# An encoder layer on one core: where the MLP's raw weights are loaded, and the order of a pair's first low part

## The chip, the cores and the metric

The kernel runs on one core of a Trainium2 chip. The metric is device time in microseconds: the median of three runs is 1814.88 us (1814.13 to 1815.59). Another execution, taken with the hardware profiler, took 1813.31 us, and its span, from the first to the last instruction, is 1811.5 us.

The engines are named as in the profile: PE multiplies matrices (PEld is its weight load), DVE and POOL work on elements, ACT computes functions and casts, and SP only issues DMA transfers. Each engine goes through its own instructions in order; semaphores hold one back until what it needs is there.

## The reference

One layer of an encoder over two sequences of 512 and 1024 tokens with 1024 features, with the same weights. Cut to what matters here:

```python
h = h + jnp.concatenate([o_attn, o_pool], axis=-1) @ w_out
m = _rmsnorm(h, norm_mlp_g)
h = h + jnp.square(jax.nn.relu(m @ w_up)) @ w_down        # the MLP: 1024 -> 4096 -> 1024
gate = jax.nn.sigmoid(_rmsnorm(h, norm_ple_g) @ w_ple_gate)
h = h + gate * (p_i @ w_ple_proj)
return _rmsnorm(h, final_norm_g)
```

Ahead of it stand an input projection, attention and a pooling mixer, which the change does not touch. All is float32.

## The kernel before

**Precision and layout.** PE multiplies in a reduced float32 format, so each operand x is split into a high part (a cast on ACT) and a low part (x minus the high part, on DVE or POOL), and each product is three matmuls: high x high, high x low, low x high (`three`). The 1536 tokens are three chunks c of 512; h is kept transposed, per chunk as four tiles `h{c}{a}` of two blocks of 128 features.

**The MLP** goes over 48 pairs: three chunks times sixteen pairs g of hidden blocks (2 x 128 hidden features each). A pair multiplies m by two columns of `w_up` by Strassen's scheme with seven products, numbered 1, 6, 2, 5, 7, 3, 4 in the order they run, each of twelve matmuls of 256 columns (px, py, pz, pq in the profile). The sums of m that the scheme needs are computed beforehand by `make_m` and go through DRAM (`mo_d`, loaded as `mo`); the sums of the weights are made for each pair by `feed` (s1 to s4 on DVE, then the split: cast on ACT, low part on POOL, L786 and L787). The results are joined into c1 and c2 (additions on DVE, L858 to L880, relu and squares on ACT, L875 to L883), and r[0] and r[1] are the high and low parts of their squares, the low parts at L886 on DVE. `down` multiplies r by two rows of `w_down` (split by `split_down`, ACT at L816, POOL and DVE at L817) in four quarters of twelve matmuls of 512 columns (pd) and adds each quarter to h (L837, DVE). The quarters of a pair run between the products of the next pair, quarter 0 after product 1.

**The order of the work** is written out by hand for PE, ACT, DVE and POOL: the text calls an instruction, and that is its place on its engine. `run` calls `after(i)` behind product i, which takes one step of several generators: of `feed` (running ahead, so that the splits of the next pair begin in `after(5)`), of `split_down`, of `raise_h`, and of the `chores`. Chores are `invert`, `finishing` of the chunk before (which ends a chunk's h and prepares the gate), and `make_m` of the chunk after. At a chunk's beginning `raise_h` multiplies h by the statistic w of the norm, in eight steps on DVE (L662).

SP's order is not written out: a transfer is issued in the place that a list scheduler gives it, "not before its turn" against PE's order, and then at run time as soon as its buffer is free. Nearly all buffers come from one pool of 49 places, so a load waits until the last reader of the place's former owner is done, and an engine that writes into a place that a DMA still reads waits for that DMA.

**Names that the prediction uses.** `wur` and `wdr` are the raw up and down weights (two tiles of 512 KB per pair), `w` their split up weights, `ws` the sums, `wd` the split down weights, `w_d` the statistic in DRAM (`sqm` is the tile in which it is computed, L646), `h_d` the place in DRAM to which `spill` writes a chunk's h until its turn comes. Before, raw up weights of the next pair are loaded in step 3 of `feed`, and its raw down weights after product 2 of the pair ahead:

```python
            for i, _ in enumerate(pr.feed()):
                if i == 3 and n + 1 < len(pairs):
                    pairs[n + 1].load_up()
                yield
```

## Time and profile before

| | |
|---|---|
| median of three runs | 1814.88 us (1814.13 to 1815.59) |
| the profiled execution | 1813.31 us, span 1811.5 us |
| mean granted clock of PE | 0.995 |
| PE busy | 1759.7 us, 97% of the span |
| DVE, POOL, ACT busy | 1260.0, 1053.7 and 939.7 us |
| the MLP in the span | from 579 us to about 1624 us |
| PE busy from 560 to 660 us | 88.3 of 100 us |
| PE busy from 930 to 1040 us | 104.6 of 110 us |
| DMA, mean over the span | 142 GB/s |

A row of a timeline has the start in us, the length, the engine, the line of the kernel, the operation, what it writes and reads by the program's names without numbers, the shape, and in square brackets how long the engine stood idle before it and on what. A row of the waits has who waited for whom, us in total, how often, and the longest. "Issue" is time in which the profile shows nothing that the engine waited for. Matmuls are pipelined: a row of twelve lasts a little longer than the time until the next twelve start, and the starts give the pace.

### The profile page before, as it was taken

The numbers are of one execution on the slowest core, as the hardware profiler recorded it, in microseconds if no ns is written. First come the engines' busy times: TensorE is split into PE (matmuls) and PEld (weight loads), VectorE is DVE, ScalarE is ACT, GpSimd is POOL, SyncE is SP. The second block draws the span as 40 slices with busy tenths as digits, with TensorE's granted clock in tenths as the row PEclk, the third lists the DMA queues.
The fourth block names the chain that finished last, engine by engine and source line by source line (L and its number), as shares of the span: only waits on it lengthen the run. The fifth ranks groups of instructions, "written<-read, shape, count | busy, mean of one in ns | idle before, by whom it ended". The sixth has DMA issues, their size and how long they took to land.

```text
span 1811.5 us, 28604 instructions
## 1 busy us (share of the span) xinstructions
PE 1759.7 (97%) x10540; PEld 1537.1 (85%) x10540; DVE 1260.0 (70%) x1843; ACT 939.7 (52%) x1854; POOL 1053.7 (58%) x923
## 2 busy tenths in 40 slices
PE   9999899999999799999999999999999999999997
PEld 7888777888868798988888889889898999888887
DVE  5677865888894677865568877876776556665655
ACT  6434455768794455655445545554455444443332
POOL 3474774535674567676656776785577666543121
PEclk9999999999999899999999999999999999999998
DMA  6333545120519335343364442556443323272102
GB/s 248 114 123 105 216 165 185 36 94 13 206 46 367 139 122 198 121 177 100 136 265 157 163 151 96 195 185 235 179 157 100 110 94 99 89 262 70 59 12 82
DMA packets 83883, 256.84 MB, mean 142 GB/s; under 512 B 9888, under 2 KB 16416, under 8 KB 83744
## 3 DMA queue, kind: packets, MB, share of 16 engines
q1 hardware_dynamic: 83744, 255.02, 39.7%
q8 instruction: 83, 1.36, 0.3%
q14 instruction: 56, 0.46, 0.1%
HBM read 195.74 MB, written 59.24 MB: 141 GB/s over the span
## 4 chain that ended last, share of the span: by engine, by line
PE 78%; DVE 7%; ACT 5%; DMA 3%; issue 3%; POOL 1%; POOLq 0%; DVEq 0%; ACTq 0%; SPq 0%
PE pd L49 25%; PE z L49 7%; PE px L49 6%; PE pz L49 6%; PE pq L49 6%; PE pg L49 6%; PE py L49 4%; PE pp L49 3%; PE o L49 3%; PE tp L53 3%; PE po L49 3%; PE S L49 3%; PE pj L49 1%; DMA wur<-in_w_up_dram 1%; DVE r L886 1%
## 5 line engine op out<-in xcount | busy, mean ns | idle before, releaser
L49 PE MATMUL pd<-r,wd 128*128 128x512 f32 x2304 | 568.5, 395 | 10.8 <-DVE r L886 10.6
L49 PEld LDWEIGHTS pd<-r,wd 128*128 128x128 f32 x2304 | 419.5, 188 | 100.3 <-DVE r L886 16.1
L787 POOL TENSOR_TENSOR w<-ws,w 128x512 fp32r<-128x512 f32 x192 | 272.5, 1423 | 217.9 <-ACT w L786 206.8
L787 POOL TENSOR_TENSOR w<-wur,w 128x512 fp32r<-128x512 f32 x144 | 212.8, 1489 | 135.4 <-ACT w L786 134.4
L837 DVE TENSOR_TENSOR h<-pd,h 128x1024 f32<-128x1024 f32 x192 | 233.5, 1216 | 76.6 <-PE pd L49 76.5
L786 ACT CAST w<-ws 128x512 fp32r<-128x512 f32 x192 | 118.5, 617 | 271.1 <-DVE ws L795 241.1
L461 POOL TENSOR_SCALAR pr<-pr,rr 128x512 f32<-128x512 f32 x160 | 111.2, 705 | 134.7 <-DVE rr L456 66.8
L49 PE MATMUL z<-w,x 128*128 128x512 f32 (+1 forms) x864 | 175.7, 359 | 0.9 <-DVE w L160 0.5
L49 PEld LDWEIGHTS pz<-mo,w 128*128 128x128 f32 x1152 | 150.7, 190 | 19.3 <-issue 11.2
L49 PEld LDWEIGHTS z<-w,x 128*128 128x128 f32 x864 | 142.9, 189 | 28.0 <-ACT w L159 2.1
L49 PE MATMUL pz<-mo,w 128*128 128x256 f32 x1152 | 153.6, 283 | 10.2 <-issue 10.2
L817 DVE TENSOR_TENSOR wd<-wdr,wd 128x512 fp32r<-128x512 f32 x96 | 102.8, 1071 | 83.1 <-ACT wd L816 76.6
L49 PE MATMUL pq<-mo,w 128*128 128x256 f32 x1152 | 153.7, 283 | 1.0 <-issue 1.0
L49 PE MATMUL px<-mo,w 128*128 128x256 f32 x1152 | 152.2, 281 | 0.0
L49 PEld LDWEIGHTS px<-mo,w 128*128 128x128 f32 x1152 | 146.5, 189 | 4.0
L49 PEld LDWEIGHTS pq<-mo,w 128*128 128x128 f32 x1152 | 144.7, 191 | 1.4 <-issue 1.3
L49 PE MATMUL pg<-hg,wg 128*128 128x512 f32 (+1 forms) x768 | 141.0, 338 | 0.2
L472 ACT CAST pt<-tp 128x512 fp32r<-128x512 f32 x160 | 88.0, 591 | 88.5 <-PE tp L53 86.8
L49 PEld LDWEIGHTS pg<-hg,wg 128*128 128x128 f32 x768 | 118.6, 188 | 17.8 <-DVE hg L1128 1.0
L817 POOL TENSOR_TENSOR wd<-wdr,wd 128x512 fp32r<-128x512 f32 x96 | 131.8, 1373 | 2.6 <-DMA w_d<-sqm 2.6
L886 DVE TENSOR_TENSOR r<-c,r 128x512 fp32r<-128x512 f32 x96 | 74.7, 783 | 74.1 <-ACT c L883 46.2
L473 DVE TENSOR_TENSOR pt<-tp,pt 128x512 fp32r<-128x512 f32 x160 | 104.0, 684 | 31.4 <-ACT pt L472 31.1
(195 smaller groups left out, 3036.2 us busy)
## 6 DMA issues: line engine op xcount, KB each, us to landing
wur<-in_w_up_dram SPq DMA_DIRECT2D x96, 512.0 KB, 4.2
wdr<-in_w_down_dram SPq DMA_DIRECT2D x96, 512.0 KB, 4.4
mo_d<-mm SPq DMA_DIRECT2D x84, 256.0 KB, 2.3
mo<-mo_d SPq DMA_DIRECT2D x42, 512.0 KB, 7.7
h_d<-h SPq DMA_DIRECT2D x16, 512.0 KB, 3.0
h<-h_d SPq DMA_DIRECT2D x16, 512.0 KB, 9.9
xn<-in_xn_dram SPq DMA_DIRECT2D x12, 512.0 KB, 6.4
qs_d<-qs SPq DMA_DIRECT2D x12, 512.0 KB, 3.0
```

Of the source, the lines that this page charges most:

```text
L49: last_pe[0] = nc.tensor.matmul(*a, **k).ins
L53: last_pe[0] = nc.tensor.transpose(*a, **k).ins
L461: gp.tensor_scalar(p, p, rr, 1.0, op0=ALU.mult, op1=ALU.mult)
L472: sc.copy(self.pt[kt][:, 0], tp)
L473: ve.tensor_tensor(self.pt[kt][:, 1], tp, as32(self.pt[kt][:, 0]), op=ALU.subtract)
L786: sc.copy(t[:, 0], x)
L787: gp.tensor_tensor(t[:, 1], x, as32(t[:, 0]), op=ALU.subtract)
L817: (gp, ve)[i].tensor_tensor(lo, self.dr[i][:, h], as32(hi), op=ALU.subtract)
L837: ve.tensor_tensor(h, pd.rearrange("p (a b) -> p a b", a=2), h, op=ALU.add)
L886: ve.tensor_tensor(self.r[i][:, 1], x, as32(self.r[i][:, 0]), op=ALU.subtract)
```

## The change

It has six parts.

1. Raw up weights of pair n+1 are loaded in step 5 of `feed` and not in step 3, raw down weights of a pair at its own beginning and not in the middle of the pair ahead. Pair 1's up weights are loaded ahead of the MLP. The casts and splits of down weights move from `after` 1, 6, 2, 5 to `after` 2, 5, 7, 3 (but for the first pair), and of each tile's two low parts POOL and DVE now take one each.
2. The low part of r[0] comes ahead of `after(4)`, whose step of `feed` makes the last sums and splits of weights; that of r[1] stays behind it.
3. In `down` the loop over f stands outside that over e, so that the first six matmuls of a quarter read r[0] and the last six r[1].
4. Chunk 0's statistic stays in SBUF (`ws[0] = acc[:, 1]`) and is not written to DRAM and read again, and chunk 0's h is raised in four double steps, from `after(2)` on.
5. Chunk 2's h is written to DRAM tile by tile as its last additions are made, not by `spill`, whose wait of 16 steps goes, so that the chores behind it begin in pair 1.
6. In `finishing` a step with a square of 1024 columns and two casts becomes two steps with half of each.

```diff
@@ make_m
-        sy.dma_start(w_d[c], acc[:, 1])
+        if c:
+            sy.dma_start(w_d[c], acc[:, 1])
+        else:
+            ws[0] = acc[:, 1]
@@ spill
-        yield from wait(16 if c == 2 else 0)
@@ heads_out
-                if d == KD - 1 and p % 2:
+                if p == 5:
+                    if d % 2:
+                        sy.dma_start(h_d[c][d // 2], hT[c][d // 2])
+                elif d == KD - 1 and p % 2:
@@ split_down
-                    (gp, ve)[i].tensor_tensor(lo, self.dr[i][:, h], as32(hi), op=ALU.subtract)
+                    (gp if i == (h.start > 0) else ve).tensor_tensor(lo, self.dr[i][:, h], as32(hi), op=ALU.subtract)
@@ down
-            for e in range(2):
-                d = 2 * a + e
-                for f in range(2):
+            for f in range(2):
+                for e in range(2):
+                    d = 2 * a + e
@@ run
+            ve.tensor_tensor(self.r[0][:, 1], c1, as32(self.r[0][:, 0]), op=ALU.subtract)
             after(4)
-            for i, x in enumerate((c1, c2)):
-                ve.tensor_tensor(self.r[i][:, 1], x, as32(self.r[i][:, 0]), op=ALU.subtract)
+            ve.tensor_tensor(self.r[1][:, 1], c2, as32(self.r[1][:, 0]), op=ALU.subtract)
@@ stream
-                if i == 3 and n + 1 < len(pairs):
+                if i == 5 and 0 < n < len(pairs) - 1:
                     pairs[n + 1].load_up()
@@ ahead of the MLP
     load_mo(0, ORDER[5]), load_mo(0, ORDER[6])
+    pairs[1].load_up()
     for a in range(4):
         load_h(0, a, h_d[0][a])
@@ finishing
-            sc.activation(sq, h, AF.Square)
-            if c == 0:
-                gate_in(0, a, True)
-            yield
+            for e in range(2):
+                sc.activation(sq[:, e], h[:, e], AF.Square)
+                if c == 0:
+                    gate_in(0, a, True, (e,))
+                yield
@@ the loop over pairs
             if c:
                 for a in range(4):
                     load_h(c, a, h_d[c][a])
-            load_ms(c)
+                load_ms(c)
...
+        if n:
+            pair.load_down()
         splits = pair.split_down()
...
-            if i == 1 and n + 1 < len(pairs):
-                pairs[n + 1].load_down()
...
-            next(splits, None)
-            if raising:
+            if n == 0 or i in (2, 5, 7, 3):
+                next(splits, None)
+            for _ in range(0 if not raising else 1 if c else 0 if i in (1, 6) else 2):
                 next(raising, None)
```

What this makes of the order shows in three places. In the names below, the digits behind a tile's letters are the chunk, then the pair or the block; the last number only tells tiles apart.

**The MLP's beginning, SP.** The transfers behind the last `mo` load; before:

```order
L56 DMA h00_6357<-h_d0_0_304 128x1024
L56 DMA h01_6359<-h_d0_1_305 128x1024
L56 DMA h02_6361<-h_d0_2_306 128x1024
L56 DMA h03_6363<-h_d0_3_307 128x1024
L647 DMA w_d0_259<-sqm0_4189 128x512
L708 DMA h_d2_0_312<-h20_5526 128x1024
L708 DMA h_d2_1_313<-h21_5528 128x1024
L708 DMA h_d2_2_314<-h22_5530 128x1024
L56 DMA wur0_10_6531<-in_w_up_dram 128x1024
L56 DMA wur0_11_6532<-in_w_up_dram 128x1024
L56 DMA w0_6556<-w_d0_259 128x512
```

And in the changed kernel:

```order
L56 DMA wur0_10_6357<-in_w_up_dram 128x1024
L56 DMA wur0_11_6358<-in_w_up_dram 128x1024
L56 DMA h00_6361<-h_d0_0_304 128x1024
L56 DMA h01_6363<-h_d0_1_305 128x1024
L56 DMA h02_6365<-h_d0_2_306 128x1024
L56 DMA h03_6367<-h_d0_3_307 128x1024
L760 DMA h_d2_0_312<-h20_5526 128x1024
L760 DMA h_d2_1_313<-h21_5528 128x1024
L760 DMA h_d2_2_314<-h22_5530 128x1024
L760 DMA h_d2_3_315<-h23_5532 128x1024
L56 DMA wdr0_10_6713<-in_w_down_dram 128x1024
```

Pair 1's up weights (wur0_1) have moved ahead of h; the statistic's two transfers (w_d0, w0) are gone; the writes of chunk 2's h follow h.

**The same place, DVE,** from the first pair's addition behind product 6 (u) on; before:

```order
L858 TENSOR_TENSOR u0_0_6558<-py0_0_6587,u0_0_6558 128x256
L662 TENSOR_TENSOR h00_6357<-h00_6357,w0_6556 128x512
L817 TENSOR_TENSOR wd0_011_6583<-wdr0_01_6346,wd0_010_6582 128x512
L662 TENSOR_TENSOR h01_6359<-h01_6359,w0_6556 128x512
L866 TENSOR_TENSOR u0_0_6558<-pz0_0_6630,u0_0_6558 128x256
L793 TENSOR_TENSOR ws0_10_6644<-wur0_11_6532 128x512
```

And now:

```order
L863 TENSOR_TENSOR u0_0_6559<-py0_0_6587,u0_0_6559 128x256
L822 TENSOR_TENSOR wd0_001_6582<-wdr0_00_6345,wd0_000_6581 128x512
L822 TENSOR_TENSOR wd0_011_6584<-wdr0_01_6346,wd0_010_6583 128x512
L665 TENSOR_TENSOR h00_6361<-h00_6361,sqm0_4189 128x512 x2
L871 TENSOR_TENSOR u0_0_6559<-pz0_0_6626,u0_0_6559 128x256
L798 TENSOR_TENSOR ws0_10_6640<-wur0_11_6358 128x512
L665 TENSOR_TENSOR h01_6363<-h01_6363,sqm0_4189 128x512 x2
```

The raises (h times w, now times sqm) come in twos behind product 2 and no longer ahead of the addition into u; one more split of down weights stands ahead of them, and one less behind.

**The second chunk's beginning, SP.** Before:

```order
L56 DMA wur1_10_10009<-in_w_up_dram 128x1024
L56 DMA wur1_11_10010<-in_w_up_dram 128x1024
L56 DMA mo1_40_10013<-mo_d1_40_288 128x1024
L56 DMA mo1_41_10014<-mo_d1_41_289 128x1024
L56 DMA h10_10033<-h_d1_0_308 128x1024
L56 DMA h11_10035<-h_d1_1_309 128x1024
L56 DMA h12_10037<-h_d1_2_310 128x1024
L56 DMA h13_10039<-h_d1_3_311 128x1024
L56 DMA w1_10041<-w_d1_260 128x512
```

And now:

```order
L56 DMA h10_10022<-h_d1_0_308 128x1024
L56 DMA h11_10024<-h_d1_1_309 128x1024
L56 DMA h12_10026<-h_d1_2_310 128x1024
L56 DMA h13_10028<-h_d1_3_311 128x1024
L56 DMA w1_10030<-w_d1_260 128x512
L56 DMA wdr1_00_10032<-in_w_down_dram 128x1024
L56 DMA wdr1_01_10033<-in_w_down_dram 128x1024
L56 DMA wur1_10_10090<-in_w_up_dram 128x1024
L56 DMA wur1_11_10091<-in_w_up_dram 128x1024
```

The next pair's up weights (wur1_1) and this pair's down weights (wdr1_0, before among the mo loads) now follow the statistic w1; wur1_0, before ahead of all mo loads, now stands behind the first two of them.

**A pair in the middle (chunk 0, pair 10), ACT and PE.** ACT between product 3 and quarter 0, before:

```order
L875 ACTIVATE c0_10_8741<-c0_10_8741 128x256
L876 ACTIVATE r0_100_8742<-c0_10_8741 128x512
L877 ACTIVATE c0_10_8741<-c0_10_8741 128x512
L786 CAST w0_11_2_8912<-wur0_110_8720 128x512
L881 ACTIVATE c0_10_8741<-c0_10_8741 128x512
L882 ACTIVATE r0_101_8743<-c0_10_8741 128x512
```

And now:

```order
L880 ACTIVATE c0_10_8739<-c0_10_8739 128x256
L881 ACTIVATE r0_100_8740<-c0_10_8739 128x512
L882 ACTIVATE c0_10_8739<-c0_10_8739 128x512
L791 CAST w0_11_2_8903<-wur0_110_8791 128x512
L821 CAST wd0_1010_8813<-wdr0_101_8735 128x512
L886 ACTIVATE c0_10_8739<-c0_10_8739 128x512
L887 ACTIVATE r0_101_8741<-c0_10_8739 128x512
```

A cast of down weights now stands between the steps for c1 and those for c2. The first matmuls of quarter 0 on PE, before (r0_100 is r[0] of the pair, r0_101 r[1]):

```order
L49 MATMUL pd0_100_8983<-r0_100_8742,wd0_1000_8762 128x512 x2
L49 MATMUL pd0_100_8983<-r0_100_8742,wd0_1001_8763 128x512
L49 MATMUL pd0_100_8983<-r0_101_8743,wd0_1010_8764 128x512 x2
L49 MATMUL pd0_100_8983<-r0_101_8743,wd0_1011_8765 128x512
L49 MATMUL pd0_100_8983<-r0_100_8742,wd0_1000_8762 128x512 x2
```

And now:

```order
L49 MATMUL pd0_100_8970<-r0_100_8740,wd0_1000_8811 128x512 x2
L49 MATMUL pd0_100_8970<-r0_100_8740,wd0_1001_8812 128x512
L49 MATMUL pd0_100_8970<-r0_100_8740,wd0_1000_8811 128x512 x2
L49 MATMUL pd0_100_8970<-r0_100_8740,wd0_1001_8812 128x512
L49 MATMUL pd0_100_8970<-r0_101_8741,wd0_1010_8813 128x512 x2
```

r[1] is first read by the seventh matmul of the quarter and no longer by the fourth.

## The prediction

> **What bounds the kernel now.** I read the page first, then the waits of the engine that carries the time, then the timeline of the stretches where it waits.
>
> ```profile
> PE 1759.7 (97%) x10540; PEld 1537.1 (85%) x10540; DVE 1260.0 (70%) x1843; ACT 939.7 (52%) x1854; POOL 1053.7 (58%) x923
> ```
>
> PE is busy in all but 51.8 of the span's 1811.5 us. The change removes no instruction of PE, so it can win only what PE waits.
>
> ```profile
> PE pd L49 <- DVE r L886: 10.6, 11, 1.8
> PE pz L49 <- issue: 10.2, 3, 9.2
> ```
>
> PE's two largest waits (us in total, times, longest) lie in the MLP: 10.6 us on the low part of r, in eleven pieces, and 10.2 us ahead of products 5 and 3, nearly all in one piece. That piece is the MLP's beginning:
>
> ```profile
> 584.71 1.57 PE L49 MATMUL pq<-mo,w 128*128 128x256 f32 x12
> 595.48 2.90 PE L49 MATMUL pz<-mo,w 128*128 128x256 f32 x12 [9.20 <-issue]
> 598.18 2.76 PE L49 MATMUL pq<-mo,w 128*128 128x256 f32 x12
> 604.34 0.96 PE L49 MATMUL pd<-r,wd 128*128 128x512 f32 x3 [1.77 <-DVE r L886]
> 606.04 2.12 PE L49 MATMUL pd<-r,wd 128*128 128x512 f32 x8 [0.74 <-DVE r L886]
> 607.99 1.60 PE L49 MATMUL py<-mo,w 128*128 128x256 f32 x12
> 609.43 1.58 PE L49 MATMUL px<-mo,w 128*128 128x256 f32 x12
> 610.85 2.93 PE L49 MATMUL pd<-r,wd 128*128 128x512 f32 x12
> 613.62 1.59 PE L49 MATMUL pz<-mo,w 128*128 128x256 f32 x12
> ```
>
> At full speed a product takes 1.43 us from start to start (607.99 to 609.43) and a quarter of a down product 2.77 (610.85 to 613.62), 0.231 per matmul. Between 584.71 and 607.99 lie 23.28 us, in which four products and one quarter run: 8.5 us of work, 14.8 us lost. The other engines tell why:
>
> ```profile
> 592.22 0.69 DVE L662 TENSOR_TENSOR h<-h,w 128x512 f32<-128x512 f32 x1 [11.38 <-DMA w<-w_d]
> 592.83 0.42 DVE L858 TENSOR_TENSOR u<-py,u 128x256 f32<-128x256 f32 x1
> 603.61 2.38 DVE L886 TENSOR_TENSOR r<-c,r 128x512 fp32r<-128x512 f32 x2
> 605.91 1.77 DVE L662 TENSOR_TENSOR h<-h,w 128x512 f32<-128x512 f32 x1
> ```
> ```profile
> 590.35 0.62 ACT L786 CAST w<-wur 128x512 fp32r<-128x512 f32 x1 [5.46 <-DMA wur<-in_w_up_dram]
> ```
> ```profile
> 569.53 11.30 DMA h<-h_d
> 580.89 9.38 DMA wur<-in_w_up_dram
> ```
> ```profile
> 585.00:590.00 5.00, 1.28 (x11) 1.08 (x10) 0.00 (x0) 0.00 (x0) 4.55 (x4) 1.00 1.03 411
> 595.00:600.00 5.00, 4.52 (x21) 4.55 (x22) 5.00 (x10) 1.50 (x3) 1.16 (x1) 0.50 0.27 107
> ```
>
> DVE stands 11.38 us on the statistic w, which goes to DRAM and back; the additions for which products 3 and 4 wait (into u and c) are behind it in DVE's order. ACT stands 5.46 us on pair 1's raw weights. The two DMA rows are pieces of the chain that ended last, the next two are windows (busy time of PE, PEld, DVE, ACT, POOL, then granted clock, DMA share, GB/s): the DMA engines are full at 411 GB/s, so 512 KB take 1.28 us, and a transfer lands 11.3 us after its issue. After the stall the granted clock is 0.50.
>
> **The change part by part: the MLP's beginning.** The sum goes against the profiled execution's 1813.31 us, 1.57 below the median. w stays in SBUF, so its write, its load and DVE's wait are gone. What is late next is a place in the pool: in the built program ACT's first cast of wd0_01 takes the buffer that h20 had, and must wait until the write of h20 has landed. This write now stands behind two loads of up weights and four of h; the first h load before landed at 569.53 + 11.30 = 580.8, so the last mo load, one transfer ahead of it, lands at 579.5. So the write lands at 579.5 + 7 x 1.28 = 588.5, the cast ends at 589.1 (0.62, as in the ACT row), and DVE goes on there, not at 592.22: 3.1 us sooner. From there to the end of the low part of r[1], DVE has 14 operations with both inputs in SBUF in either kernel (now one split, eight raises, s1 to s3, two r; before, two splits and seven raises), and four additions out of PSUM instead of five. Before, that took from 592.22 to 605.99, 13.8 us. I take 13.8 - 0.4 and come to 602.5. With f outside e this low part is the operand of the 8th matmul of twelve, not of the 5th, and 5 x 0.231 = 1.2 us follow it: the quarter ends at 603.7 instead of 607.99. **4.3 us won.**
>
> The bounds come from DVE's own rows: one raise takes 0.69 us, another 1.77, where POOL works beside it.
>
> ```profile
> 603.98 3.15 POOL L787 TENSOR_TENSOR w<-ws,w 128x512 fp32r<-128x512 f32 x2 [0.84 <-ACT w L786]
> ```
>
> With nothing beside it the chain takes 14 x 0.6 (592.22 to 592.83) + 4 x 0.35 = 9.8 us; then the two products after the stall, at half clock (595.48 to 598.18 and on to 600.74, 5.3 us), and ACT's three steps behind them hold the end at some 599.9, a gain of 6.9. POOL has five operations left in this stretch; if each costs DVE the 1.1 us between the two raises, the chain takes 15.3 us, and 2.4 us are won. I stay at 4.3, since the stretch before had the same mixture. The Trainium skill (SBUF — State Buffer, "Who interferes with whom") says that a DVE operation with two SBUF inputs and a GpSimd operation that reads SBUF contend, and that the order of issue decides which of them blocks; the two raises agree with it. Counted by that rule for all 14 operations, this term would be a loss; where it could decide is a rival below.
>
> **The other two chunks' beginnings.** PE loses this at the second, and nearly the same at the third:
>
> ```profile
> 920.00:925.00 5.00, 5.00 (x29) 4.29 (x29) 2.92 (x4) 4.31 (x9) 3.74 (x3) 1.00 1.03 409
> ```
> ```profile
> 931.00 1.75 DVE L662 TENSOR_TENSOR h<-h,w 128x512 f32<-128x512 f32 x1 [6.47 <-DMA w<-w_d]
> ```
> ```profile
> 937.59 1.67 PE L49 MATMUL pz<-mo,w 128*128 128x256 f32 x12 [0.52 <-issue]
> 939.73 1.67 PE L49 MATMUL pq<-mo,w 128*128 128x256 f32 x12 [0.47 <-issue]
> 947.22 2.12 PE L49 MATMUL pd<-r,wd 128*128 128x512 f32 x8 [0.72 <-DVE r L886]
> 1286.31 1.64 PE L49 MATMUL pz<-mo,w 128*128 128x256 f32 x12 [0.52 <-issue]
> 1288.45 1.67 PE L49 MATMUL pq<-mo,w 128*128 128x256 f32 x12 [0.49 <-issue]
> 1296.00 2.13 PE L49 MATMUL pd<-r,wd 128*128 128x512 f32 x8 [0.76 <-DVE r L886]
> ```
>
> That is 1.71 + 1.77 = 3.5 us. Again DVE waits 6.47 us for w in a full queue (409 GB/s). From the first mo load to w SP now issues 20 loads of 512 KB, not 22: the down weights of this pair and the up weights of the next, four loads, follow w, and this pair's two up-weight loads come in among mo. So w lands 2 x 1.28 = 2.6 us sooner, more than each of the waits behind it. They may go altogether (3.5), or, if a weight load is now late instead, stay (0). I take **2.7**, nearer to the first, because the loads put behind w are needed only some 7 us later, when products 1, 6 and 2 and a quarter (3 x 1.43 + 2.77) have run.
>
> **The low part of r in the middle of the chunks.** Of the 10.6 us, 1.77 + 0.74 + 0.72 + 0.76 are counted above; 6.6 are left, 3.7 of them in three pieces:
>
> ```profile
> 990.34 2.14 PE L49 MATMUL pd<-r,wd 128*128 128x512 f32 x8 [0.75 <-DVE r L886]
> 1013.37 1.89 PE L49 MATMUL pd<-r,wd 128*128 128x512 f32 x7 [1.46 <-DVE r L886]
> 1036.50 2.15 PE L49 MATMUL pd<-r,wd 128*128 128x512 f32 x8 [1.52 <-DVE r L886]
> ```
> ```profile
> 1028.75 1.06 ACT L1142 ACTIVATE sqg<-h 128x1024 f32<-128x1024 f32 x1
> 1029.71 1.32 ACT L1126 ACTIVATE hg<-h,gple_sb 128x512 fp32r<-128x512 f32 x2
> ```
> ```profile
> 1035.12 1.32 DVE L886 TENSOR_TENSOR r<-c,r 128x512 fp32r<-128x512 f32 x1 [1.61 <-ACT c L883]
> ```
>
> In each it is r[1] that is late, behind ACT's chain of c, and ACT has one step of `finishing`, 1.06 + 1.32 us, ahead of c. The change cuts this step in two halves of some 1.2 us and makes a period of seven steps one of eight, so that the heavy step no longer falls in the same place of each pair. The new order of the matmuls gives 3 x 0.231 = 0.69 us more; but a cast of down weights (0.62, 0.52 from start to start) now stands between the chains of c1 and c2 and takes 0.52 of it away. I take **2.0** of the 6.6; the bounds are 5.5 (the three pieces and some of the rest) and -2 (the moved casts and splits stall two or three pairs that were quiet).
>
> **At no cost.** The raw weights' loads still come early enough:
>
> ```profile
> DMA to landing us min/median/max: 3.3/4.2/9.6
> ```
>
> In the built program, the second up-weight load of pair n+2 waits for product 3 of pair n, and is first needed after product 2 of pair n+1, 4 x 1.43 + 2 x 2.77 = 11.3 us later, against 4.2 (9.6 in the full queue). Without that cover ACT would stand, in order, ahead of c. The shorter wait in `spill` lets the steps of `invert` and `make_m(1)` start in pair 1, where DVE waits for PE; the twelve more ACT instructions lie in ACT's idle half. Sum: 4.3 + 2.7 + 2.0 = 9.0 us, or 1805.9 from the median.
>
> **The rivals.** *The start keeps its stall* (0.17): the queue is as full as before, the write of h20 lands late, and a contended DVE eats the 3.1 us. For it: DMA share 1.03 to the end of the stretch; against it: w's two transfers are gone. Then 1 to 4.5 us are left, 1812. *All waits of the beginnings go* (0.08): the buffer comes free early and nothing holds DVE; up to 14.8 + 3.5 us less small remainders, about 16, 1799. *Nothing moves* (0.10): the DMA engine is the bound there whatever the order, and the pool's places, not the place in the program, set the loads: within 2 us, 1815. *Slower* (0.10): after product 7 DVE now has the split of down weights ahead of the addition into c1.
>
> ```profile
> L837 DVE TENSOR_TENSOR h<-pd,h 128x1024 f32<-128x1024 f32 x192 | 233.5, 1216 | 76.6 <-PE pd L49 76.5
> ```
>
> Until product 3 ends there are 2.77 + 1.43 = 4.2 us, for an addition into c2 (0.42), s2, the split and a step of the chores (0.69 each) and the addition into h (1.22): 3.7 us alone, but 6.9 where POOL stretches three of them to 1.77. Then c1, c2 and r are 2.7 us late, of which I put 1.8 on PE, an estimate: quiet pairs show no wait on r, so they have some slack. Seven or more such pairs more than eat the sum, twelve make 1814.9 + 21.6 - 9.0 = 1827. Against it: the total of DVE's work per pair is unchanged, and only pairs with chores on DVE can show it.
>
> **How the numbers follow.** The likeliest case (0.55) is the sum, with its bounds taken together some 5.5 to 13.5 us: 1801 to 1809.5; 1806. A measurement of this kernel can tell about 0.2%, 3.6 us, from no change. Faster by more than that, below 1811.3: 0.55 + 0.08 + 0.10 of the first rival = 0.73. The same: 0.07 of it and 0.10 = 0.17. Slower: 0.10. The range of 8 in 10 takes in the kept start and some of the better case: 1799.5 to 1813.
>
> **What would show it.** Right: DVE's wait on w is gone from the beginning, ACT waits there until about 588.5 into the span for an h_d write, the piece of 9.2 us shrinks to about 6, and py of pair 1 starts near 603.7; at the second chunk DVE's wait falls from 6.5 to about 4 us and the pieces of 0.5 are gone; the waits on r outside the beginnings fall from 6.6 to under 5 us. Wrong: ACT waits on wur or wdr in the middle of the chunks, new waits of PE on c or r in pairs with chores, or no wait of ACT or DVE at the beginning at all.

## The result, and the profile after

The changed kernel takes 1883.99 us (1883.18 to 1884.80), against 1814.88 us for the kernel before: a ratio of 1.0382 (95% interval 1.0367 to 1.0397). It is 69 us slower, where 9 us less were forecast. The profiled execution's span is 1882.2 us, 70.7 longer than before's. Line numbers of the changed kernel stand five or so higher than before's: L786 is now L791, L787 L792, L817 L822, L837 L842, L874 L879, and the low parts of r, L886, are now L889 (r[0]) and L891 (r[1]).

The page's row of busy times, and the waits of PE (in all, how often, longest):

```profile
PE 1786.8 (95%) x10540; PEld 1548.9 (82%) x10540; DVE 1299.2 (69%) x1843; ACT 938.4 (50%) x1862; POOL 1057.0 (56%) x923
```
```profile
PE pd L49 <- DVE r L891: 36.2, 27, 3.1
PE pq L49 <- DVE c L875: 9.9, 5, 4.7
PE pd L49 <- DVE r L889: 8.7, 9, 3.2
PE pz L49 <- issue: 7.2, 1, 7.2
```

PE has the same 10540 matmuls. It idles 95.4 us of its span, 43.6 more than before, and is busy 27.1 us more. Much of the second follows from the first. The timeline and the window around the longest wait behind the MLP's beginning show how (the window's columns are the busy times of PE, PEld, DVE, ACT and POOL, then the granted clock, the DMA share and GB/s):

```profile
1275.73 2.90 PE L49 MATMUL pq<-mo,w 128*128 128x256 f32 x12 [4.66 <-DVE c L875]
1278.42 4.19 PE L49 MATMUL pd<-r,wd 128*128 128x512 f32 x12
```
```profile
1275.00:1280.00 5.00, 4.27 (x16) 4.01 (x17) 3.72 (x6) 1.66 (x3) 3.01 (x3) 0.50 0.28 105
```

Behind 4.66 us of idleness the granted clock is 0.50; the product takes 2.69 us to the next start instead of 1.43, and the quarter is shown with 4.19 us instead of 2.95. The mean granted clock is 0.986 against 0.995; 0.009 of the span, 17 of the 27 us, is an estimate of what the slow clock adds. The rest I put down, without having shown it, to the tails of rows that end in a wait: a quarter is shown with 2.95 us though the next group starts after 2.77, and the difference counts as busy only where nothing follows.

The waits are spread. From the start of one product 6 to that of the next, 46 pairs take 987.5 us before and 1060.9 now; 31 of them took less than 21.3 us, now 17 do: the seven from 797 us on, one at 1310 us and the nine from 1476 us on. None of these 17 has a step of a chore on DVE. So I compare such a quiet pair in both kernels. Before, on PE (product 3, then quarter 0) and DVE:

```profile
873.65 1.57 PE L49 MATMUL pz<-mo,w 128*128 128x256 f32 x12
...
880.68 2.93 PE L49 MATMUL pd<-r,wd 128*128 128x512 f32 x12
```
```profile
871.53 0.68 DVE L795 TENSOR_TENSOR ws<-ws,wur 128x512 f32<-128x512 f32 x1
873.85 1.22 DVE L837 TENSOR_TENSOR h<-pd,h 128x1024 f32<-128x1024 f32 x1 [1.64 <-PE pd L49]
875.26 0.42 DVE L874 TENSOR_TENSOR c<-pz,u 128x256 f32<-128x256 f32 x1 [0.19 <-PE pz L49]
...
880.05 0.69 DVE L886 TENSOR_TENSOR r<-c,r 128x512 fp32r<-128x512 f32 x1 [1.72 <-ACT c L883]
```

And now, on PE, DVE, ACT and POOL:

```profile
871.84 1.57 PE L49 MATMUL pz<-mo,w 128*128 128x256 f32 x12
...
878.86 3.12 PE L49 MATMUL pd<-r,wd 128*128 128x512 f32 x12
```
```profile
869.80 0.67 DVE L800 TENSOR_TENSOR ws<-ws,wur 128x512 f32<-128x512 f32 x1
871.68 1.36 DVE L822 TENSOR_TENSOR wd<-wdr,wd 128x512 fp32r<-128x512 f32 x1 [1.21 <-ACT wd L821]
872.97 1.21 DVE L842 TENSOR_TENSOR h<-pd,h 128x1024 f32<-128x1024 f32 x1
874.11 0.41 DVE L879 TENSOR_TENSOR c<-pz,u 128x256 f32<-128x256 f32 x1
...
876.99 1.79 DVE L806 TENSOR_TENSOR ws<-wur,wur 128x512 f32<-128x512 f32 x1
879.34 1.16 DVE L891 TENSOR_TENSOR r<-c,r 128x512 fp32r<-128x512 f32 x1 [0.56 <-ACT c L888]
```
```profile
870.51 0.62 ACT L791 CAST w<-ws 128x512 fp32r<-128x512 f32 x1 [4.44 <-DVE ws L800]
871.04 0.61 ACT L821 CAST wd<-wdr 128x512 fp32r<-128x512 f32 x1
...
876.77 0.61 ACT L821 CAST wd<-wdr 128x512 fp32r<-128x512 f32 x1
877.29 0.63 ACT L886 ACTIVATE c<-c 128x512 f32<-128x512 f32 x1
```
```profile
876.94 1.30 POOL L792 TENSOR_TENSOR w<-wur,w 128x512 fp32r<-128x512 f32 x1 [4.44 <-ACT w L791]
878.19 1.75 POOL L822 TENSOR_TENSOR wd<-wdr,wd 128x512 fp32r<-128x512 f32 x1
```

Measured from the start of product 3, the addition into c1 started at 1.61 us before and starts at 2.27 now; r[1]'s low part ended at 7.09 and ends at 8.66, 1.57 later. Behind product 7 DVE used to be idle until the quarter's result came. Now it makes the sum (869.80), waits 1.21 us, because the cast that its split needs stands on ACT behind the cast of that very sum, splits for 1.36 beside POOL, and only then adds the quarter into h and product 3 into c1: 0.66 late. On ACT the moved cast (876.77) adds its 0.52 ahead of c2. At the end POOL's moved split (878.19) stretches the low part from 0.69 to 1.16.

The wait for a cast is not new, its place is. Before, DVE stood 76.6 us in 35 pieces on casts of down weights, and in all of them behind product 2, where nothing was late for it: in the quiet pair its split there waits 2.05 us and takes 1.38, and DVE still has to wait for product 5 before the next addition into u (869.65).

```profile
866.87 1.38 DVE L817 TENSOR_TENSOR wd<-wdr,wd 128x512 fp32r<-128x512 f32 x1 [2.05 <-ACT wd L816]
```

This eats a slack. Before, the low part of r[1] was the operand of the fifth matmul of a quarter and ended 0.86 us ahead of it (880.68 + 4 x 0.231 - 880.74). The new order of the matmuls gives 0.69 more: 0.86 + 0.69 - 1.57 = 0. Quiet pairs just get by. In a pair with chores PE pays for a further step on DVE, as in this one (of the 29 pairs over 21.3 us, 23 have a chore's step or a raise of h on DVE; four of the other six wait for weights, which come next):

```profile
638.94 1.37 DVE L822 TENSOR_TENSOR wd<-wdr,wd 128x512 fp32r<-128x512 f32 x1 [1.26 <-ACT wd L821]
640.23 0.68 DVE L609 TENSOR_TENSOR sqm<-sqm,sqm 128x512 f32<-128x512 f32 x1
640.83 1.21 DVE L842 TENSOR_TENSOR h<-pd,h 128x1024 f32<-128x1024 f32 x1
641.97 0.41 DVE L879 TENSOR_TENSOR c<-pz,u 128x256 f32<-128x256 f32 x1
...
644.92 1.79 DVE L806 TENSOR_TENSOR ws<-wur,wur 128x512 f32<-128x512 f32 x1
646.63 1.78 DVE L609 TENSOR_TENSOR sqm<-sqm,sqm 128x512 f32<-128x512 f32 x1
648.34 0.68 DVE L891 TENSOR_TENSOR r<-c,r 128x512 fp32r<-128x512 f32 x1
```
```profile
649.07 1.44 PE L49 MATMUL pd<-r,wd 128*128 128x512 f32 x5 [1.20 <-DVE r L891]
```

Two chore steps (L609) are in the way here, one behind product 7 and one between the two low parts of r. PE's waits on c are of another kind. DVE and ACT now wait for raw up weights (ACT stood there once, for 5.5 us, before). Behind these two rows of waits stand SP's longest wait between 1184 and 1192 us, its issue of such a load, and DVE and PE in that pair, in which PE lost 3.05 us on c:

```profile
DVE ws L798 <- DMA wur<-in_w_up_dram: 17.7, 5, 6.4
```
```profile
ACT w L791 <- DMA wur<-in_w_up_dram: 29.3, 8, 7.8
```
```profile
SPq L636 <- POOL mm L634: 6.7, 3, 3.4
```
```profile
1190.59 0.91 SPq L56 DMA_DIRECT2D wur<-in_w_up_dram  x2
```
```profile
1197.40 1.21 DVE L798 TENSOR_TENSOR ws<-wur 128x512 f32<-128x512 f32 x1 [4.85 <-DMA wur<-in_w_up_dram]
...
1200.20 0.41 DVE L875 TENSOR_TENSOR c<-pq,u 128x256 f32<-128x256 f32 x1
```
```profile
1200.76 1.68 PE L49 MATMUL pq<-mo,w 128*128 128x256 f32 x12 [3.05 <-DVE c L875]
```

DVE waits for these weights until 1197.40, and the addition into c for which PE stands 3.05 us is behind that in DVE's order. ACT's cast of them (1196.09) waits 6.02 us, from 1190.1 on, before SP had even issued the load. SP's loads themselves waited 0.2 us in this stretch; this one stood in SP's order behind writes of m's sums (L636), which wait for POOL.

### The profile page after: what moved, and what is told of

Same layout as the page of the kernel before. It is cut to its first block, busy times and chain, and to the rows that moved or that the text cites. A ratio compares the mean times of both kernels' runs of the same rounds, so it can differ in the third digit from the quotient of the medians.

```text
span 1882.2 us, 28639 instructions
## 1 busy us (share of the span) xinstructions
PE 1786.8 (95%) x10540; PEld 1548.9 (82%) x10540; DVE 1299.2 (69%) x1843; ACT 938.4 (50%) x1862; POOL 1057.0 (56%) x923
## 3 DMA queue, kind: packets, MB, share of 16 engines
q8 instruction: 83, 1.36, 0.3%
## 5 line engine op out<-in xcount | busy, mean ns | idle before, releaser
L49 PE MATMUL pd<-r,wd 128*128 128x512 f32 x2304 | 586.5, 400 | 48.5 <-DVE r L891 36.2
L792 POOL TENSOR_TENSOR w<-ws,w 128x512 fp32r<-128x512 f32 x192 | 284.7, 1498 | 164.5 <-ACT w L791 147.6
L792 POOL TENSOR_TENSOR w<-wur,w 128x512 fp32r<-128x512 f32 x144 | 190.4, 1322 | 259.4 <-ACT w L791 246.9
L842 DVE TENSOR_TENSOR h<-pd,h 128x1024 f32<-128x1024 f32 x192 | 233.0, 1214 | 147.5 <-PE pd L49 147.5
L791 ACT CAST w<-ws 128x512 fp32r<-128x512 f32 x192 | 118.2, 616 | 290.7 <-DVE ws L800 219.2
L822 DVE TENSOR_TENSOR wd<-wdr,wd 128x512 fp32r<-128x512 f32 x96 | 105.9, 1103 | 62.5 <-ACT wd L821 37.0
L822 POOL TENSOR_TENSOR wd<-wdr,wd 128x512 fp32r<-128x512 f32 x96 | 145.1, 1512 | 6.2 <-DVE c L885 6.2
L821 ACT CAST wd<-wdr 128x512 fp32r<-128x512 f32 x192 | 118.5, 618 | 5.0 <-DMA h_d<-h 4.0
```

Source lines behind the costliest of these rows:

```text
L49: last_pe[0] = nc.tensor.matmul(*a, **k).ins
L791: sc.copy(t[:, 0], x)
L792: gp.tensor_tensor(t[:, 1], x, as32(t[:, 0]), op=ALU.subtract)
L821: sc.copy(hi, self.dr[i][:, h])
L822: (gp if i == (h.start > 0) else ve).tensor_tensor(lo, self.dr[i][:, h], as32(hi), op=ALU.subtract)
L842: ve.tensor_tensor(h, pd.rearrange("p (a b) -> p a b", a=2), h, op=ALU.add)
```

## The experiments

Theory S says that the moved casts and splits of down weights are the loss. Its rivals are R, the step of `after(4)` that now stands between the two low parts, and U, the later load of up weights.

**e1: casts, splits and loads of down weights back in their places.**

```diff
-            if n == 0 or i in (2, 5, 7, 3):
-                next(splits, None)
+            next(splits, None)
-        if n:
-            pair.load_down()
+            if i == 1 and n + 1 < len(pairs):
+                pairs[n + 1].load_down()
```

> The changed kernel, but the casts and splits of down weights again behind products 1, 6, 2 and 5, and their loads again in the middle of the pair ahead. Theory S (the moved casts and splits make c1 late on DVE and c2 late on ACT, so r[1] has no slack left: in the quiet pair of the changed kernel its low part ends 8.66 us after product 3 starts, against 7.09 before): nearly all waits of PE on r go, those on c (9.9 us and the slow clock behind them) stay: about 1825 us, r[1] low again near 7.1 us after product 3. Theory R (the step of after(4) that now stands between the two low parts holds r[1]): no more than 10 us are regained, 1873 or above. Theory U (up weights loaded two steps later hold ACT and DVE): 1870 or above.

Measured: 1822.01 us, 1.0035 (1.0025 to 1.0046) of before. 62 of the 69 us are back, and the low part of r[1] in the quiet pair ends 7.09 us after product 3 starts, as before. Theory S holds as a whole, although the loads of down weights have gone back with the steps; e5 and e16 below leave these loads where the change has them.

**e2: both low parts behind `after(4)` again.**

```diff
-            ve.tensor_tensor(self.r[0][:, 1], c1, as32(self.r[0][:, 0]), op=ALU.subtract)
             after(4)
+            ve.tensor_tensor(self.r[0][:, 1], c1, as32(self.r[0][:, 0]), op=ALU.subtract)
```

> The changed kernel, but both low parts of r again behind after(4). Theory R: nearly all waits on r go, 1825 us or less. Theory S: only the seven or eight pairs gain in which a chore's step on DVE stood between the two low parts and ended after ACT (648, 720, 794, 967, 1062, 1353 and 1423 us into the span), some 1.5 us each: about 1872 us. Theory U: 1880.

Measured: 1868.23 us, 1.0292 (1.0277 to 1.0307). R alone isn't the loss, but this part costs 15.8 us here, somewhat more than S allowed.

**e3: up weights loaded in step 3 again.**

```diff
-                if i == 5 and 0 < n < len(pairs) - 1:
+                if i == 3 and n + 1 < len(pairs):
-    pairs[1].load_up()
```

> The changed kernel, but the raw up weights of the next pair again loaded in step 3 of feed, pair 1's among them. Theory U: DVE and ACT no longer wait for raw up weights (47 us in 13 pieces now), and most of the 69 us goes: 1830 us or less. Theory S: only PE's waits on c (9.9 us in five pieces, and the slow clock behind them) go: about 1870 us. Theory R: 1870 as well.

Measured: 1876.22 us, 1.0337 (1.0322 to 1.0353). 7.8 us; U as the main cause falls.

**e4: all three undone.**

> All three of these undone at once; what is left of the change is the order of the matmuls in a quarter, the statistic kept in SBUF, the early writes of chunk 2's h, the halved step of finishing and the engines of the low parts. Every theory in which the three are the whole loss: 1806 to 1815 us. If one of the other parts costs something: above 1820.

Measured: 1814.36 us, 0.9994 (0.9984 to 1.0003). The three hold the whole loss, and what is left of the change is worth nothing as it stands.

**e5, e6: which step of the four.** The steps ran behind products 2, 5, 7 and 3; in e5 they run behind 6, 2, 5, 3, in e6 behind 6, 2, 5, 7.

```diff
-            if n == 0 or i in (2, 5, 7, 3):
+            if n == 0 or i in (6, 2, 5, 3):      # e5;  e6: (6, 2, 5, 7)
```

> The changed kernel with the steps of the down weights behind products 6, 2, 5 and 3 and no longer 2, 5, 7 and 3; everything else as changed. Theory S7 (the split on DVE behind product 7, with the addition into h behind it, holds c1, and all of r with it): most of the 62 us that e1 regained comes back, 1835 us or less. Theory S3 (the cast on ACT behind product 3 holds the chain of c2, and POOL's split beside it stretches the low part of r[1] from 0.69 to 1.15 us): c1 is 0.66 us sooner in a quiet pair, but r[1] is late by the other 0.98, and at most half comes back: 1853 or above.

> The changed kernel with the steps of the down weights behind products 6, 2, 5 and 7; the one behind 7 stays, the one behind 3 goes. Theory S3: 1840 us or less. Theory S7: r[1] gains 0.98 us in a quiet pair, but c1 stays late: 1853 or above. If both hold about alike, e5 and e6 both come out near 1845.

Measured: e5 1835.46 us, 1.0106 (1.0088 to 1.0125); e6 1820.73 us, 1.0033 (1.0020 to 1.0046). Read as planned, both S7 and S3 were borne out, which can't be: 49 and 63 us are more than the 69 together. The two edits overlap. The steps are taken in order, and their splits are on POOL, DVE, DVE and POOL, so e6 did not only free product 3: the step behind product 7 became the fourth, POOL's, and DVE's split went from behind product 7 to behind product 5 there too.

**e9, e13, e14: the step behind product 3, taken apart.** In e9 ACT's last cast goes one step ahead, in e13 POOL's last split goes to the end of the pair, in e14 both.

```diff
                 for h in halves:
                     hi, lo = (x[:, h] for x in self.wd[i])
-                    sc.copy(hi, self.dr[i][:, h])
+                    if (i, h) != (1, halves[1]):                                   # e9, e14
+                        sc.copy(hi, self.dr[i][:, h])
+                    if (i, h) == (1, halves[0]):
+                        sc.copy(self.wd[1][0][:, halves[1]], self.dr[1][:, halves[1]])
+                    if i and h.start:                                              # e13, e14
+                        yield
```

> The changed kernel, but ACT's last cast of down weights is made in the step behind product 7, directly behind the third; POOL's split that reads it stays behind product 3. Tells the two halves of the step behind product 3 apart. If ACT's cast ahead of the chain of c2 (0.52 us) is what costs: near e6, 1820 to 1832 us. If POOL's split beside the low part of r[1] (0.69 to 1.15 us) is: little regained, 1860 or above. About half each: 1840 to 1855.

> The changed kernel, but the last split of a pair's down weights is made on POOL at the end of the pair, behind its other work there; its cast on ACT stays behind product 3. If POOL's split holds the low part of r[1] (in e9 and in the changed kernel it ends 0.55 us after that split, whenever it starts): the low part takes 0.69 and not 1.15 us in quiet pairs, r[1] is 0.47 us sooner, and half or more of the 69 us is regained, 1850 or below. If POOL's split is no cause either: 1870 or above.

> e9 and e13 together: the last cast behind product 7, the last split at the end of the pair, so nothing of the down weights is left behind product 3. If cast and split cover each other (taking one away leaves the other as the last to end): 1820 to 1830 us, like e6, and r[1]'s low part 1.2 us sooner than in the changed kernel. If the loss comes from something else in that place (the phase of the steps, the place of the first three): 1850 or above.

Measured: e9 1883.49 us, 1.0379 (1.0365 to 1.0394); e13 1876.53, 1.0341 (1.0327 to 1.0355); e14 1867.27, 1.0288 (1.0274 to 1.0302). So 0.5, 7.5 and 16.7 us: cast and split do cover each other, but with both gone 52 us of the loss are still there, and the expectation of 1820 to 1830 falls. So does that of e13: in its quiet pair the low part takes 0.69 us and ends 8.12 us after product 3 starts, 0.54 sooner, as expected, but the kernel stays above 1850. Why e9 regains nothing shows on POOL and DVE of a quiet pair of e9 (L826 is the split of down weights, L895 the low part of r[1]):

```profile
878.00 1.74 POOL L826 TENSOR_TENSOR wd<-wdr,wd 128x512 fp32r<-128x512 f32 x1
```
```profile
878.62 1.67 DVE L895 TENSOR_TENSOR r<-c,r 128x512 fp32r<-128x512 f32 x1
```

The low part starts sooner, 6.94 us after product 3 (which starts at 871.68 here) and not 7.50, but takes 1.67 us instead of 1.16 and ends 0.55 us after POOL's split (880.29 and 879.74), as it does in the changed kernel (880.50 and 879.94).

**e16: DVE's split away from product 7, ACT's casts where the change has them.** DVE now makes the first two splits, POOL the last two.

```diff
-                    (gp if i == (h.start > 0) else ve).tensor_tensor(lo, ...)
+                    (ve, gp)[i].tensor_tensor(lo, ...)
```

> The changed kernel, but DVE makes the first two splits (behind products 2 and 5, where it had its two before) and POOL the last two (behind 7 and 3). ACT's four casts stay behind 2, 5, 7 and 3. If DVE's split behind product 7 is the main cause (it stands 1.21 us on ACT's cast, takes 1.36 beside POOL's split, and the addition into h and that into c1 are behind it): 1840 us or less, like e5. If the casts or POOL's splits in their late places are: 1860 or above.

Measured: 1832.42 us, 1.0092 (1.0077 to 1.0108). 51.6 us are back, from two splits that change places: DVE's goes from behind product 7 to behind 2, POOL's the other way. In its quiet pair DVE is again idle ahead of the addition into h, and c1 is added when product 3 ends:

```profile
854.68 0.68 DVE L800 TENSOR_TENSOR ws<-ws,wur 128x512 f32<-128x512 f32 x1
857.01 1.23 DVE L842 TENSOR_TENSOR h<-pd,h 128x1024 f32<-128x1024 f32 x1 [1.65 <-PE pd L49]
858.42 0.43 DVE L879 TENSOR_TENSOR c<-pz,u 128x256 f32<-128x256 f32 x1 [0.18 <-PE pz L49]
```

The low part of r[1] ends 8.01 us after product 3 starts there, and not 8.66. For these casts DVE waits even longer in e16 than in the changed kernel (85.5 us against 37.0 put down to ACT, 8.1 against 25.5 to "issue"), but nearly all of it behind product 2 again.

With e5 (49 us, by another edit that takes the same split away) this settles the place of the main cause. All seven kernels in which DVE splits behind product 7 take 1867 us or more (the changed kernel, e2, e3, e9, e13, e14 and e7 below), and every other kernel here 1836 or less. One thing goes along with it: POOL's first split stands behind product 2 in the seven and elsewhere in all others, and no run moved it alone. That DVE's is the one that costs rests on the rows above, in which c1 is late behind it.

**e7: the down weights' part alone, on the kernel before** (places, engines and loads as in the change).

> The kernel before with this one part alone: the casts and splits of down weights behind products 2, 5, 7 and 3, their engines alternated, their loads at the pair's own beginning. Theory S, if the parts add up: 1815 + 62 = 1877 us. If the step of after(4) between the low parts and the late up weights are needed for the loss: 1845 or less. A quarter here still needs r[1] at its fourth matmul and not at its seventh (0.69 us), which speaks for the upper number.

Measured: 1888.08 us, 1.0404 (1.0388 to 1.0419). Alone it costs 73 us, more than the whole change: the others win 4 beside it. Here no pair takes less than 21.3 us, and the quiet ones take 21.4 to 21.6: without the new order of the matmuls and its 0.69 us they don't get by, as the account of the slack says.

**e8, e10, e11, e12: is anything left to win?** e8 is e4 with pair 1's up weights ahead of h; e10 is e8 with `spill` and its wait as before, in place of the early writes of chunk 2's h; e11 is the kernel before with the beginning alone; e12 is e6 with the other two parts undone.

```diff
-                if i == 5 and 0 < n < len(pairs) - 1:      # e8, e10, e11, e12
+                if i == 3 and 0 < n < len(pairs) - 1:
     def spill(c):                                           # e10
+        yield from wait(16 if c == 2 else 0)
```

> e4 with pair 1's up weights loaded ahead of h (as the change does), the others in step 3 of feed: what is left of the change is the MLP's beginning, the order in a quarter, the early writes of chunk 2's h and the halved step. In e4 DVE stood 3.15 us and ACT 4.24 us on those weights, and the beginning (product 7 to the end of the first quarter) took 20.9 us, against 23.3 before and 19.5 in the changed kernel. If they are what e4 lacks: 1.4 to 1.7 us less than e4's 1814.4, about 1812.8. If the loads ahead of h delay h and its raise: 1814 or above.

> e8 with spill and its wait of 16 steps as before, so that the chores of chunk 0 start two pairs later and fall otherwise against the pairs. In e4, which was no faster than before though its beginning was, pairs 3, 21 and 28 lost 1.7 to 4.6 us, where chores' steps on DVE and POOL held r; before lost less there and more in pairs 17 to 19. If the earlier start of the chores brought that: 1809 to 1811.5 us. If not: 1812.5 to 1815.

> The kernel before with the MLP's beginning alone: the statistic of chunk 0 kept in SBUF, h raised in double steps from after(2) on, pair 1's up weights loaded ahead of h. The beginning (product 7 to the end of the first quarter) took 23.3 us before, 19.5 in the changed kernel, 20.9 in e4. If nothing is given back later: 2.4 to 3.8 us less than before, 1811 to 1812.5. If w was never the last to be waited for: 1815.

> e6 (down weights loaded at the pair's own beginning, split behind products 6, 2, 5 and 7) with the order of r's low parts and the loads of up weights undone, as in e8. e6 was 6 us above before. If those two parts are the rest of the loss: 1811 to 1815 us, like e8. If the step behind product 7 or the later load of down weights costs by itself: 1818 or above.

Measured: e8 1813.55 us, 0.9992 (0.9983 to 1.0002); e10 1812.77, 0.9986 (0.9977 to 0.9995); e11 1813.95, 0.9992 (0.9983 to 1.0001); e12 1829.72, 1.0077 (1.0063 to 1.0090). In e11's trace the beginning takes 20.1 us instead of 23.3 (product 7 at 586.55, the quarter's end at 606.64), but the total moved only by about 1.1, less than expected; e8 and e11 can't be told from no change. In e11's profiled execution the 46 pairs behind the beginning took 989.1 us against 987.5 before; why stays open. e12 went the wrong way, for a reason that I had not thought of. With up weights issued sooner and down weights at the pair's own beginning, ACT waits for the latter (in e6 this row reads 11.7 us in six pieces):

```profile
ACT wd L821 <- DMA wdr<-in_w_down_dram: 53.2, 15, 7.4
```

e10 is faster by 0.14%, yet with bad pairs: the one from 1054 us on takes 24.13 us, and 22.49 before. POOL and DVE there, behind product 3 of that pair in e10 (L548 and L552 are steps of a chore that finishes a norm):

```profile
1070.10 1.28 POOL L790 TENSOR_TENSOR w<-wur,w 128x512 fp32r<-128x512 f32 x1 [3.31 <-ACT w L789]
```
```profile
1072.69 1.48 DVE L552 TENSOR_TENSOR dgg<-id_sb,rhg 128x512 fp32r<-128x512 f32 x2 [4.43 <-POOL rhg L548]
1074.08 0.42 DVE L883 TENSOR_TENSOR c<-pq,u 128x256 f32<-128x256 f32 x1
```

POOL gets to its part of the chore only behind that split, which itself waits for a cast; DVE stands 4.43 us on it, with the addition into c2 behind. The halved step of `finishing` had made four steps more, and so put all later chores in another place of the pair.

**e15: e10 with those four steps taken from the wait behind them.**

```diff
-        yield from wait(6)
+        yield from wait(2)
```

> e10 with the wait of finishing cut from 6 steps to 2, so that what follows the halved steps (four more than before) starts in the same place of a pair as before. In e10 pairs 17 to 19, 24, 34 and 35 lose some 6 us less than before, but pairs 21 and 28 some 6 us more, where steps of the norm and of make_m(2) on POOL and DVE hold r. If that is the phase: 1807 to 1810 us. If not: 1812 to 1815, like e10.

Measured: 1802.65 us, 0.9935 (0.9921 to 0.9948). This is 12.4 us faster than before and 81 us faster than the change. e10, which differs from it by these steps of waiting alone, is 10 us slower, so that much hangs on the chores' places. The same chore now starts behind product 6, as it did before; DVE still waits 3.64 us for POOL there, but PE waits for nothing in that pair, which takes 22.42 us. PE's waits on r, 10.6 us before, are down to one:

```profile
PE pz L49 <- issue: 9.5, 3, 7.3
...
PE pd L49 <- DVE r L888: 1.4, 1, 1.4
```

**e17, e18: two terms by themselves.** e17 is the kernel before with the halves and `wait(2)`; e18 is e15 with the order of the matmuls in a quarter as before.

> The kernel before with the halved step of finishing alone, and its wait cut from 6 steps to 2 so that what follows keeps its place. e15 was 12.4 us faster than before, of which its beginning (some 3.8) and the third chunk's and second chunk's beginnings (1.3) are another part. If the halves bring the rest: 1807 to 1809 us. If the order in the quarter or the engines of the splits bring it: 1812 or above.

> e15 with the order of the matmuls in a quarter as before (e outside f). With r[1] read by the seventh matmul and not by the fourth, 0.69 us of a late r[1] is hidden, in some six pairs and three beginnings: 1805 to 1808 us, if that order is worth what the prediction gave it. If r[1] is in time in e15 anyway: 1802 to 1804.

Measured: e17 1813.62 us, 0.9991 (0.9982 to 1.0000); e18 1806.65 us, 0.9956 (0.9943 to 0.9968). The halves alone are worth about 1.7 us, which is at the edge of what can be told from nothing, and so don't bring the rest of e15's gain; the order, against e15, is worth 4.0.

## Why the prediction was wrong

**The MLP's beginning, 4.3 us won: right in the trace.** In the changed kernel, on PE and ACT:

```profile
586.15 1.59 PE L49 MATMUL pq<-mo,w 128*128 128x256 f32 x12
594.94 2.90 PE L49 MATMUL pz<-mo,w 128*128 128x256 f32 x12 [7.20 <-issue]
...
605.64 1.58 PE L49 MATMUL py<-mo,w 128*128 128x256 f32 x12
```
```profile
589.81 0.62 ACT L821 CAST wd<-wdr 128x512 fp32r<-128x512 f32 x1 [3.99 <-DMA h_d<-h]
```

From product 7 to the quarter's end it takes 19.5 us instead of 23.3, so 3.8 are won, and in the way forecast: a cast waits for an h_d write (to 589.8; I had 588.5), and DVE's chain to the end of the low part of r[1] behind it takes 13.9 us (590.46 to 604.31; I had 13.4). Only 2.35 us show in the absolute time, since this execution reached product 7 at 586.15, 1.4 us later than before's; other kernels came there between 585.21 and 587.67, also e17, which changes nothing ahead of it (585.80). As a gain of the whole kernel the term is not shown: e11, which has this part alone, is 1.1 us faster, within the noise.

**The other beginnings, 2.7 us: wrong.** w came sooner in the changed kernel (one wait for it, 2.8 us), but the first pairs of the second and third chunks took 24.64 and 25.49 us instead of 23.54 and 23.60, now for r (PE stands 3.06 and 3.05 us on it). With the old order of loads e15 wins 0.6 and 0.7 us there (22.92 and 22.87 against 23.54 and 23.60), so the win, as far as there is one, isn't that of the loads.

**The low part of r, 2.0 us: the step that failed.** The term took the moved casts and splits for 0.52 us of ACT's time per pair and, at its lower bound of -2, for "two or three pairs that were quiet". They cost 62 us (e1, with their loads), and DVE's split behind product 7 is the main part (51.6 us in e16, 49 in e5). The sum has no price for that split: it counted the cast on ACT and left out that DVE's split stands behind product 7 and there waits for its cast, ahead of the addition into c1. What the term counts as a gain had the right sign where it can be measured by itself (order 4.0; halves 1.7, at the edge of the noise and with a shorter wait than the change has).

**The rival "slower" (0.10, 1827 us): the right mechanism, mis-sized.** It named the place, DVE's split behind product 7 ahead of the addition into c1, and set 3.7 us of work against a window of 4.2. What was missing is the wait of 1.21 us for ACT in this place: DVE's sum, ACT's cast of it, ACT's next cast, DVE's split are a chain across two engines. With it and the split at 1.36 the quiet pair alone comes to 4.7 (869.47, the addition into c2, to 874.18). The row that told it was there before the run: ACT's first cast behind that product waited 4.42 us for DVE's sum in the quiet pair before as well, so a second cast behind it could not be early.

```profile
872.30 0.62 ACT L786 CAST w<-ws 128x512 fp32r<-128x512 f32 x1 [4.42 <-DVE ws L795]
```

It also gave quiet pairs "some slack" and chore pairs a share of 1.8 us. The slack was 0.86 + 0.69 us, and the moved steps used all of it in quiet pairs, so that 29 of the 46 pairs, not twelve, took over 21.3 us, on average 24.1 (a quiet pair takes 21.2 to 21.3). It was right that only pairs with more work than the quiet ones would show it; there are just more of them. Two of the signs that the prediction gave for being wrong came true: ACT waits on wur in the middle of the chunks (29.3 us), and PE has new waits on c and r in pairs with chores.

**At no cost: wrong for the loads and for the steps added.** The loads were not early enough (7.8 us by e3). I set their lead, from the place in the program to the use, against the time from issue to landing (4.2 us, 9.6 in the full queue); but SP issues in order, and in the pairs of `make_m` the issue itself is late, behind writes that wait for POOL. The halved step's additional ACT instructions (eight by the pages, 1862 against 1854, and not twelve) cost nothing that shows by themselves (e17), but the steps that carry them shift the chores behind, which is the 10 us between e10 and e15. I had seen that the steps move and counted it as a gain.

**Not in the sum at all: the low part of r[0] ahead of `after(4)`,** 15.8 us by e2 in this kernel. I had priced only the order of the matmuls. In the quiet pair before, the sum in `after(4)` ran in 0.68 us (877.04) while ACT was still at work on c1 and c2. In the changed kernel it starts just after POOL's split of up weights (L792, 876.94), takes 1.79 us beside it and stands ahead of the low part of r[1].

The prices of e2 and e3 and the 51.6 of e16 add up to more than the loss, because a pair is held by the later of its causes.

## What to carry to other kernels

A moved instruction has the place of what it reads as well as its own: before putting an operation in an idle gap, follow its operand to the engine that makes it, and ask whether that one comes out of the same gap. Slack is one account for all parts of a change; sum what each takes from the same deadline, here the low part of r[1] at its matmul of the quarter, before any is put down as free. And where work is dealt out in steps, adding steps shifts all that follows: keep the count (four steps less of waiting were worth 10 us in e15), or look anew at what each chore then stands ahead of.

## What the runs showed of the hardware

The contention of DVE and POOL is not a stretch by some factor but a wait for the end. In the changed kernel 45 of the 48 sums L806 start while an operation of POOL that began sooner is running, and each ends 0.54 or 0.55 us after it. Of the 48 low parts of r[1], 41 start so, and 39 of them end 0.55 or 0.56 us after POOL's operation. Of the other two, one starts so near POOL's end that it takes its 0.69 us anyway; the other starts in the same moment as POOL's (648.34), and there DVE's takes 0.68 us and POOL's 1.84. So the length of such an operation of DVE, 0.68 to 1.80 us, is set by how much of POOL's is left. The Trainium skill (SBUF — State Buffer, "Who interferes with whom") says that such a DVE operation and a GpSimd read exclude one another and that the order of issue decides; these rows agree, and e9 shows its consequence: starting DVE's operation 0.56 us sooner (against product 3) moved its end by 0.05. What has to be moved then is POOL's operation: in e13, which did that, the low part of the quiet pair is back at 0.69 us and the kernel 7.5 us faster, against 0.5 in e9.
